# A gated delta layer on one core: conv taps read from PSUM, and VectorE in GpSimd's place for the weights' low parts and the silu products

## The chip, the core and the metric

The kernel runs on one core of one Trainium2 chip. The metric is device time in microseconds (us) of one execution. Before the change the median of three runs is 1683.63 us (1683.09 to 1684.1).

## The reference

Two decoder blocks run one after the other on 256 tokens of width 1024. The first prepends 16 meta tokens (272 columns in the kernel) and has two layers: a gated delta layer and an mLSTM layer, each followed by a feed-forward part with a short conv. The second has a feed-forward part, three mixers and another feed-forward part. The change touches the gated delta layer alone:

```python
def gated_deltanet(h, valid, w_in, conv_w, a_log, dt_bias, norm_w, w_out):
    proj = h @ w_in
    qkv = jax.nn.silu(causal_depthwise_conv(proj[..., :o1], conv_w)).astype(f32)
    z = proj[..., o1:o2]
    beta = jax.nn.sigmoid(proj[..., o2:o3])
    g = -jnp.exp(a_log) * jax.nn.softplus(proj[..., o3:] + dt_bias)
    ...
    sol = lax.linalg.triangular_solve(a_mat, rhs, left_side=True, lower=True)
    ...
    _, o = lax.scan(step, S0, xs)
    o = rms_norm(o, norm_w) * jax.nn.silu(z)
    return o.reshape(B, L, GDN_VAL_DIM) @ w_out
```

`w_in` is 1024 x 6176: 1024 columns for the queries, 1024 for the keys, 2048 for the values, 2048 for the gate z, and 32 for beta and g. The conv has 4 taps and runs along the tokens, for each channel by itself.

## The kernel before

Activations lie with channels on the partitions and tokens along the free axis. A product with a weight matrix keeps float32 accuracy with three float32r matmuls: each weight piece is split into a high part `wh` (a rounding copy by ScalarE) and a low part `wl` (the rest, a subtraction by GpSimd or VectorE), the activations likewise, and TensorE adds high by high, high by low and low by high in PSUM (`linear_g`, line 403). A load (`wload`, line 355) is one DMA of 512 KB into `wraw`, the copy that makes `wh`, and the subtraction that makes `wl`. There are three buffers each of `wraw`, `wh` and `wl`, so a load starts when the one three before it has been used.

In the delta layer `linear_g` is called for 256 columns at a time: two PSUM tiles `ps`, two loads of four 128-row pieces each, 24 matmuls a load. The pool has two `ps` buffers. 32 loads make the queries, keys and values (`gdn_proj`, line 971) in four groups of heads, 16 loads make z (`gdn_z`), and a small one the gates. In this layer GpSimd makes `wl` in two halves of 128x512, but for the first two loads, which `embed` prefetches for VectorE.

`conv4` (line 955) turns a `ps` tile into silu of the conv: ScalarE copies `ps` to `cx` in SBUF and writes the last tap to `cy`; VectorE adds the other three taps from `cx` (128x271, 128x270, 128x269); ScalarE takes tanh (`cth`); and the product (1 + tanh) y goes to `kv`, by VectorE in one instruction for the channel tiles 0 to 13 and by GpSimd in two (`cth`, then `kv`) for tiles 14 to 31. The `ps` buffer is free again when ScalarE has read it twice.

Beside the projections run the chunks of the delta rule, on four lanes: `unit_kq` normalises keys and queries (small VectorE chains `rq_*`, then `kqtok` on ScalarE), `gdn_pre` makes the decays (`dp`, `kk`, `BA`), `gdn_core` inverts a triangular matrix by levels (`wy_inverse`: matmul `yp`, ScalarE `Y`, matmuls `w`, VectorE `RT`, then `zp`, `Z`, `r2p`) and updates the state, `gdn_onorm` normalises the output (`on`, `otp`), and `gdn_tail` does the last 16 tokens for all heads (`wp`, `up`, `vnp`, `rsp`). When all is done, the output projection `ps<-og` begins. It ends the layer.

The order of TensorE's instructions is fixed when the program is built: each of these pieces is a generator that yields the tiles it waits for, and a planner (`Threads`, line 114) with costs for each engine picks the piece that could go on first by its reckoning. The other engines run in the order that the tile scheduler gives them. Every engine takes its instructions strictly in that order. `seg` counts the later parts of the network and is 0 in the delta layer; `ordered` and `mixing` are false there.

Of the kernel before, what the change touches and what calls it, by code (L numbers as in the profile page):

```python
# [8 lines left out]
F32 = mybir.dt.float32  # L9
# [5 lines left out]
ALU = mybir.AluOpType  # L15
# [6 lines left out]
T = S + NM  # L22
KD = D // 128
# [62 lines left out]
class Event:  # L86


    def __init__(self):
        self.on = False  # L90
        self.v = None
# [117 lines left out]
class Kern:  # L209
    def __init__(self, ctx, tc, ins, out):  # L210
        self.tc, self.nc, self.ctx = tc, tc.nc, ctx
        nc = tc.nc
        self.th = Threads()
        self.mem_done, self.half = Event(), Event()
        self.pause = [Event() for _ in range(3)]
        self.mwt = {}
        self.ready = {}
        self.V, self.A, self.PE, self.G = (self.th.engine(*e) for e in (
            ("V", nc.vector), ("A", nc.scalar), ("PE", nc.tensor), ("G", nc.gpsimd)))
        self.SY = nc.sync  # L220
        self.i = ins
        self.out = out

        self.const = self.pool(ctx, "const", 1)
        self.p_raw = self.pool(ctx, "praw", 3)
        self.p_hl = self.pool(ctx, "phl", 3)
        self.p_x = self.pool(ctx, "px", 8)
        self.p_h = self.pool(ctx, "ph", 14)
        self.p_s = self.pool(ctx, "psm", 2)
        self.p_t = self.pool(ctx, "ptiny", 2)  # L230
        self.lane = None
        self.ordered = False
        self.mixing = False
        self.near_load = self.seg = 0
        self.mid = None
        self.gctx = ExitStack()
        self.pp = self.pool(self.gctx, "pq", 2, space=PSUM)
        self.p_v = self.pool(self.gctx, "pkvg", 8)
        self.p_l = self.pool(self.gctx, "plane", 1)
        self.p_lp = self.pool(self.gctx, "planep", 1, space=PSUM)  # L240
# [37 lines left out]
        return t  # L278

    def ps(self, shape=(128, T), name="ps"):  # L280
        return self.pp.tile(list(shape), F32, tag="pp", name=name)

    def pcore(self, shape=(128, 4, 128), name="pcs"):
        return self.pc.tile(list(shape), F32, tag="pc", name=name)
# [72 lines left out]
    def wload(self, w, k0, nk, c0, nc_, pieces=1, late=None, own=None, eng=None):  # L357

        key = w.tensor.name, k0, c0
        if key in self.ready:  # L360
            return self.ready.pop(key)
        tile = own or (lambda name, dt: (self.p_raw if name == "wraw" else self.p_hl).tile(
            [128, nk, nc_], dt, tag=name, name=name))
        r = tile("wraw", F32)
        self.A.ahead = self.V.ahead = self.G.ahead = True
        h, l = tile("wh", F32R), tile("wl", F32R)
        self.SY.dma_start(
            r[:], w[k0 * 128:(k0 + nk) * 128, c0:c0 + nc_].rearrange("(k p) c -> p k c", p=128))
        self.nload = getattr(self, "nload", 0) + 1
        every = POOL_EVERY[self.seg]  # L370
        if eng is not None:
            pass
        elif not self.ordered or self.mixing or self.nload <= self.near_load or every and self.nload % every == 0:
            eng, pieces = self.nc.gpsimd if self.ordered or self.mixing else self.G, 2
        else:
            eng = self.V
        sub = [(slice(k, k + nk // pieces), slice(None)) for k in range(0, nk, nk // pieces)] if nk >= pieces else [
            (slice(None), slice(c, c + nc_ // pieces)) for c in range(0, nc_, nc_ // pieces)]
        inst = self.A.copy(h[:], r[:])

        def low():
            for a, b in sub:
                eng.tensor_tensor(l[:, a, b], r[:, a, b], h[:, a, b].bitcast(F32), ALU.subtract)  # L383

        if late is None:
            low()
        else:
            if self.ordered:
                self.order(inst)
            late.append(low)  # L390
        self.A.ahead = self.V.ahead = self.G.ahead = False
        return h, l
# [406 lines left out]
    def embed(self):  # L799

        self.hst = self.cst([128, KD, T], name="hst")
        self.hs = [self.hst[:, k, :] for k in range(KD)]
        f = self.xt
        ss = self.cst([128, 2, 3], name="ss0")
        st = self.tiny([128, 2, 6], "ss1")
        mv = self.tiny([128, 2], "ss2")
        w = self.i["gdn_w_in"][0]
        X = self.xslots()

        def prefetch(*a):  # L810
            late = []
            self.ready[w.tensor.name, a[0], a[2]] = self.wload(w, *a, eng=self.V, late=late)
            return late

        with self.tc.manual_schedule(engines={mybir.EngineType.DVE}):
            self.V.memset(ss[:], 1.0)
            self.V.memset(ss[:, 1, 1:2], 0.0)
            for t in (2, 0):
                for n in range(2):
                    P = TT[t][1]  # L820
                    junk = self.vslot((128, 512), F32, "junk")
                    self.act(junk[:P], f[t][n][:P], AF.Square, accum_out=ss[:P, n, t:t + 1])
            for n in range(2):
                self.V.bn_stats(st[:, n, :], f[1][n][:])
            self.lane = "u1"
            p = self.plane("warm", (128, 512))
            for _ in range(35):
                self.mm(p[:], self.zero[:, :128], self.zero[:])
            self.lane = None
            self.V.bn_aggr(mv[:], st[:])  # L830
            self.stt(ss[:, 0, 1:2], mv[:, 0:1], mv[:, 0:1], mv[:, 1:2], ALU.mult, ALU.add)
            self.ts(ss[:, 0, 1:2], ss[:, 0, 1:2], float(D), ALU.mult)
            self.tt(ss[:, 0, :], ss[:, 0, :], ss[:, 1, :], ALU.add)
            self.ss = ss
            r = self.rsqrt_small([128, 3], ss[:, 0, :], D, EPS)
            rd = self.vslot((128, 3, 128), F32, "rd")
            for t, (o, P) in enumerate(TT):
                self.ts(rd[:P, t, :P], self.ident[:P, :P], r[:P, t:t + 1], ALU.mult)
            self.columns(self.norms, 0)
            low = {1: prefetch(0, KD, 6144, 32), 3: prefetch(0, 4, 1024, 256), 6: prefetch(4, 4, 1024, 256)}  # L840
            self.masks()
            for k in range(KD):
                self.lane = k % 4
                p = self.plane("xp", (128, T))
                for t, (o, P) in enumerate(TT):
                    self.mm(p[:, o:o + P], f[t][k // 4][:P, (k % 4) * 128:(k % 4) * 128 + 128], rd[:P, t, :P], t == 0, True)
                self.act(X[k][0], p[:], AF.Copy, scale=self.pv(k))
                self.stt(X[k][1], p[:], self.pv(k), X[k][0].bitcast(F32), ALU.mult, ALU.subtract)
                for fn in low.get(k, ()):
                    fn()  # L850
            self.lane = None
        self.th.add([self.residual()])
        return X
# [101 lines left out]
    def conv4(self, ps, ct, out):  # L955

        w = lambda j: self.pv(PV_GC + j * 32 + ct)
        y = self.sm(name="cy")
        x = self.p_l.tile([128, T], F32, tag="cx", name="cx", bufs=3)
        self.A.copy(x[:], ps)  # L960
        self.act(y[:], ps, AF.Copy, scale=w(3))
        for s in (1, 2, 3):
            self.stt(y[:, s:], x[:, :T - s], w(3 - s), y[:, s:], ALU.mult, ALU.add)
        th = self.sm(name="cth", tag="th")
        self.act(th[:], y[:], AF.Tanh, scale=0.5)
        if ct >= 14:
            self.tt(th[:], th[:], y[:], ALU.mult, self.G)
            self.tt(out, th[:], y[:], ALU.add, self.G)
        else:
            self.stt(out, th[:], 1.0, y[:], ALU.add, ALU.mult)  # L970

    def gdn_proj(self, X, g):
        W = self.i["gdn_w_in"][0]
        qs, ks, v0, v1 = (self.vslot() for _ in range(4))
        for base, dst in ((1024 + g * 256, ks), (g * 256, qs), (2048 + g * 512, v0), (2304 + g * 512, v1)):
            yield from self.linear_g(W, base, 256, KD, X, T, lambda m, p: self.conv4(p, base // 128 + m, dst[:, m, :]))
        tl = slice(256, T)
        self.G.tensor_copy(self.kqtail[:, 0, 2 * g:2 * g + 2, :], ks[:, :, tl])
        self.G.tensor_copy(self.kqtail[:, 1, 2 * g:2 * g + 2, :], qs[:, :, tl])
        for n, v in enumerate((v0, v1)):  # L980
            self.G.tensor_copy(self.vtail[:, 4 * g + 2 * n:4 * g + 2 * n + 2, :], v[:, :, tl])
        return qs, ks, (v0, v1)
# [1468 lines left out]
```

## Time and profile before

| | us |
|---|---|
| median of three runs | 1683.63 |
| the profiled execution, its own time | 1685.52 |
| its span, first to last instruction | 1683.7 |
| span up to the first projection `ps<-xhl` | 24.3 |
| from there to the first `ps<-og` (the delta layer) | 341.2 |
| the rest | 1318.2 |

The profile names instructions as `output<-inputs` with their shapes. PE is TensorE's matmuls, PEld its weight loads, DVE VectorE, ACT ScalarE, POOL GpSimd. A row's busy time is that of a group; "idle before" is the time in which its engine stood still just before it, and the releaser is what ended that. Nearly all compute instructions bear line 190, that of the helper that records them, so groups are told apart by tile names.

### The profile page before, as it was taken

The page shows a single profiled execution, that of the slowest core. Times are in us where ns is not written, and L with a number is a line of the kernel's source. Part 1 is how long each engine was busy: PE and PEld are TensorE (multiplying, and loading weights), DVE is VectorE, ACT ScalarE, POOL GpSimd, SP SyncE. Part 2 cuts the span into 40 slices and gives each one's busy share as a digit, 9 for nine tenths or more (in the row PEclk, how much of TensorE's full clock was granted, in tenths as well). Part 3 has the DMA queues.
Part 4 walks back from the last instruction along what each step waited for, and adds up shares of the span by engine and source line. Part 5 has one row for each costly group of instructions (what it writes and reads, how often), then busy time and mean ns, then how long its engine had stood idle before and what let it go on. Part 6 is the DMA issues. An engine that isn't in the chain of part 4 may idle for free.

```text
span 1683.7 us, 31234 instructions
## 1 busy us (share of the span) xinstructions
PE 1557.9 (93%) x11939; PEld 1470.2 (87%) x11939; DVE 1141.3 (68%) x2284; ACT 936.2 (56%) x1893; POOL 576.6 (34%) x531
## 2 busy tenths in 40 slices
PE   8889888999799997999799998999997899999999
PEld 6778778899799996888788998999986789999987
DVE  5788878766988758448977667554659564466643
ACT  4567766655566544447566646454544655564542
POOL 3674554320200002450334441112265547612221
PEclk9899999999999999999899999999998999999999
DMA  5331221236355553335346554556654335656664
GB/s 157 88 89 53 75 63 55 72 110 196 113 171 169 175 175 101 91 114 151 118 156 190 170 181 150 176 178 197 184 149 128 101 93 151 186 158 184 184 191 150
DMA packets 239100, 235.40 MB, mean 140 GB/s; under 512 B 11510, under 2 KB 226406, under 8 KB 238950
## 3 DMA queue, kind: packets, MB, share of 16 engines
q1 hardware_dynamic: 238326, 231.86, 46.1%
q8 instruction: 94, 1.54, 0.4%
q0 software_dynamic: 496, 1.41, 0.3%
q14 instruction: 56, 0.46, 0.1%
q10 hardware_dynamic: 128, 0.13, 0.0%
HBM read 232.32 MB, written 1.05 MB: 139 GB/s over the span
## 4 chain that ended last, share of the span: by engine, by line
PE 39%; DVE 9%; DMA 3%; ACT 3%; issue 1%; POOL 1%; ACTq 0%; POOLq 0%; DVEq 0%
PE ps L190 31%; PE pst L190 5%; ACT wh L190 1%; DVE wl L190 1%; PE memp L190 1%; DVE fy L190 1%; DVE rq_a L190 1%; DMA wraw<-in_ffn_w_up_dram 1%; DMA wraw<-in_ml_w_out_dram 1%; DVE rq_y L190 1%; DMA wraw<-in_mem_w_kv_dram 1%; POOL wl L383 1%; DVE qtok L190 1%; DVE qsq L190 1%; PE rsp L190 0%
## 5 line engine op out<-in xcount | busy, mean ns | idle before, releaser
L190 ACT CAST wh<-wraw 128x1024 fp32r<-128x1024 f32 (+2 forms) x436 | 447.9, 1029 | 392.2 <-PE ps L190 249.8
L190 PE MATMUL ps<-xhl,wh 128*128 128x272 f32 (+2 forms) x3280 | 639.8, 295 | 19.7 <-DVE py L190 8.3
L383 POOL TENSOR_TENSOR wl<-wraw,wh 128x512 fp32r<-128x512 f32 (+3 forms) x262 | 333.4, 1296 | 666.4 <-ACT wh L190 616.1
L190 PEld LDWEIGHTS ps<-xhl,wh 128*128 128x128 f32 x3280 | 514.5, 192 | 25.9 <-DVE py L190 8.7
L190 PE MATMUL ps<-xhl,wl 128*128 128x272 f32 (+2 forms) x1640 | 465.1, 288 | 0.8 <-POOL wl L383 0.8
L190 DVE TENSOR_TENSOR wl<-wraw,wh 128x1024 fp32r<-128x1024 f32 (+3 forms) x239 | 289.1, 1210 | 180.8 <-ACT wh L190 176.2
L190 PEld LDWEIGHTS ps<-xhl,wl 128*128 128x128 f32 x1640 | 312.2, 192 | 1.2 <-POOL wl L383 1.2
L190 PE MATMUL ps<-xr,wh 128*128 128x256 f32 (+2 forms) x1216 | 225.3, 293 | 25.0 <-DVE py L190 23.0
L190 POOL TENSOR_TENSOR wl<-wraw,wh 128x512 fp32r<-128x512 f32 x132 | 172.4, 1327 | 162.7 <-ACT wh L190 154.5
L190 PEld LDWEIGHTS ps<-xr,wh 128*128 128x128 f32 x1216 | 191.8, 197 | 27.7 <-DVE py L190 18.2
L190 PE MATMUL ps<-hh,wh 128*128 128x256 f32 (+1 forms) x1056 | 190.8, 283 | 0.0
L190 PE MATMUL ps<-xr,wl 128*128 128x256 f32 (+2 forms) x608 | 164.1, 291 | 1.1 <-DVE wl L190 1.1
L190 PEld LDWEIGHTS ps<-hh,wh 128*128 128x128 f32 x1056 | 163.1, 188 | 0.0
L190 PE MATMUL ps<-hh,wl 128*128 128x256 f32 (+1 forms) x528 | 149.8, 284 | 0.4 <-DVE wl L190 0.4
L190 PEld LDWEIGHTS ps<-xr,wl 128*128 128x128 f32 x608 | 114.0, 196 | 1.6 <-DVE wl L190 1.5
L190 PEld LDWEIGHTS ps<-hh,wl 128*128 128x128 f32 x528 | 99.6, 189 | 0.6 <-DVE wl L190 0.6
L190 DVE SCALAR_TENSOR_TENSOR cy<-cx,pvt,cy 128x271 f32<-128x271 f32 (+2 forms) x96 | 74.5, 779 | 13.5 <-ACT cy L190 12.5
L190 DVE SCALAR_TENSOR_TENSOR fy<-ps,pvt,fy 128x256 f32<-128x256 f32 (+2 forms) x128 | 62.4, 488 | 17.4 <-ACT fy L190 16.0
L190 DVE TENSOR_TENSOR hh<-fy,hh 128x256 fp32r<-128x256 f32 (+1 forms) x88 | 63.8, 728 | 11.7 <-ACT hh L190 11.6
L190 DVE TENSOR_TENSOR py<-ps,rstd 128x256 f32<-128x256 f32 (+2 forms) x96 | 39.9, 423 | 37.8 <-PE ps L190 37.5
L190 POOL MEMSET mvt<- 128x4 f32 x4 | 0.4, 102 | 182.9 <-PE ps L190 182.9
L190 ACT CAST hh<-fy 128x256 fp32r<-128x256 f32 (+1 forms) x88 | 35.7, 408 | 38.4 <-DVE fy L190 37.8
(537 smaller groups left out, 2650.8 us busy)
## 6 DMA issues: line engine op xcount, KB each, us to landing
wraw<-in_ffn_w_up_dram SPq DMA_DIRECT2D x88, 512.0 KB
wraw<-in_ffn_w_gu_dram SPq DMA_DIRECT2D x88, 512.0 KB
wraw<-in_ffn_w_down_dram SPq DMA_DIRECT2D x79, 512.0 KB
wraw<-in_gdn_w_in_dram SPq DMA_DIRECT2D x48, 512.0 KB
wraw<-in_w_in_dram SPq DMA_DIRECT2D x41, 512.0 KB
wraw<-in_ml_w_in_dram SPq DMA_DIRECT2D x24, 512.0 KB
wraw<-in_gdn_w_out_dram SPq DMA_DIRECT2D x16, 512.0 KB
wraw<-in_ml_w_out_dram SPq DMA_DIRECT2D x8, 512.0 KB
```

Of the source, the lines that this page charges most:

```text
L190: r = f(*args, **kw)
L383: eng.tensor_tensor(l[:, a, b], r[:, a, b], h[:, a, b].bitcast(F32), ALU.subtract)
```

## The change

Four edits. `conv4` no longer copies `ps` to `cx`: the three taps read `ps` itself; and all 32 products are made by VectorE in one instruction. In `wload`, `wl` is made by VectorE in one piece of 128x1024 wherever `seg` is 0 and no engine was named; later parts keep their rules. `gdn_proj` calls `linear_g` for 128 columns at a time: one `ps` tile, one load of eight 128-row pieces of 128 columns, 24 matmuls; the prefetched loads follow. And before each such tile the generator yields the key of the buffer that it takes (`free`), so that the planner reckons with the time at which the tile two before was read.

```diff
     def ps(self, shape=(128, T), name="ps"):
-        return self.pp.tile(list(shape), F32, tag="pp", name=name)
+        t = self.pp.tile(list(shape), F32, tag="pp", name=name)
+        self.taken.append(t.tensor.name)
+        return t
+
+    def free(self, t):
+
+        n = self.taken.index(t.tensor.name)
+        key = f"pp{n % 2}"
+        self.th.bank[key] = self.taken[n - 2] if n > 1 else None
+        return key
...
-            eng, pieces = self.nc.gpsimd if self.ordered or self.mixing else self.G, 2
+            eng, pieces = (self.nc.gpsimd, 2) if self.ordered or self.mixing else (self.V, 1) if self.seg == 0 else (self.G, 2)
...
-            low = {1: prefetch(0, KD, 6144, 32), 3: prefetch(0, 4, 1024, 256), 6: prefetch(4, 4, 1024, 256)}
+            low = {1: prefetch(0, KD, 6144, 32), 3: prefetch(0, KD, 1024, 128), 6: prefetch(0, KD, 1152, 128)}
...
-        x = self.p_l.tile([128, T], F32, tag="cx", name="cx", bufs=3)
-        self.A.copy(x[:], ps)
         self.act(y[:], ps, AF.Copy, scale=w(3))
         for s in (1, 2, 3):
-            self.stt(y[:, s:], x[:, :T - s], w(3 - s), y[:, s:], ALU.mult, ALU.add)
+            self.stt(y[:, s:], ps[:, :T - s], w(3 - s), y[:, s:], ALU.mult, ALU.add)
         th = self.sm(name="cth", tag="th")
         self.act(th[:], y[:], AF.Tanh, scale=0.5)
-        if ct >= 14:
-            self.tt(th[:], th[:], y[:], ALU.mult, self.G)
-            self.tt(out, th[:], y[:], ALU.add, self.G)
-        else:
-            self.stt(out, th[:], 1.0, y[:], ALU.add, ALU.mult)
+        self.stt(out, th[:], 1.0, y[:], ALU.add, ALU.mult)
...
-            yield from self.linear_g(W, base, 256, KD, X, T, lambda m, p: self.conv4(p, base // 128 + m, dst[:, m, :]))
+            for m in range(2):
+                ps = self.ps((128, T))
+                yield [self.free(ps)]
+                yield from self.linear_g(W, base + m * 128, 128, KD, X, T,
+                                         lambda _, p: self.conv4(p, base // 128 + m, dst[:, m, :]), [ps])
```

Three places show what this does to the order of instructions. The first is VectorE at the head of the layer, while the gates' chain (`lp`, ending in `gg`) runs between the first convs. Before:

```order
L190 TENSOR_TENSOR ba<-ba,db 128x3x16
L190 TENSOR_SCALAR lp<-lp 128x96
L190 RECIPROCAL lp<-lp 128x96
L190 SCALAR_TENSOR_TENSOR cy<-cx,pvt,cy 128x271
L190 TENSOR_TENSOR lp<-lp 128x96
L190 SCALAR_TENSOR_TENSOR cy<-cx,pvt,cy 128x270
L190 TENSOR_TENSOR lp<-lp 128x96
L190 SCALAR_TENSOR_TENSOR cy<-cx,pvt,cy 128x269
L190 TENSOR_SCALAR lp<-lp 128x96
```

With the change:

```order
L190 TENSOR_TENSOR ba<-ba,db 128x3x16
L190 TENSOR_TENSOR wl<-wraw,wh 128x1024
L190 SCALAR_TENSOR_TENSOR cy<-ps,pvt,cy 128x271
L190 TENSOR_SCALAR lp<-lp 128x96
L190 SCALAR_TENSOR_TENSOR cy<-ps,pvt,cy 128x270
L190 RECIPROCAL lp<-lp 128x96
L190 SCALAR_TENSOR_TENSOR cy<-ps,pvt,cy 128x269
L190 TENSOR_TENSOR wl<-wraw,wh 128x1024
L190 TENSOR_TENSOR lp<-lp 128x96
```

The taps read `ps`, and two `wl` now stand in VectorE's queue between the first step of the gates and the rest of their chain.

The second is GpSimd in the same layer, from the last of the constants (`lvl`) on. Before:

```order
L190 CAST lvl<-ctmp 128x4x128 x2
L190 TENSOR_TENSOR wl<-wraw,wh 128x512 x8
L190 COPY kqtail<-kv 128x32
L190 TENSOR_TENSOR wl<-wraw,wh 128x512 x2
L190 COPY kqtail<-kv 128x32
L190 TENSOR_TENSOR wl<-wraw,wh 128x512 x4
L190 TENSOR_TENSOR cth<-cth,cy 128x272
L190 TENSOR_TENSOR kv<-cth,cy 128x272
```

With the change:

```order
L190 CAST lvl<-ctmp 128x4x128 x2
L190 COPY kqtail<-kv 128x32 x2
L190 COPY vtail<-kv 128x32 x2
L190 COPY kqtail<-kv 128x32
L190 AFFINE_SELECT BA<-BA 128x256
L190 CAST Br<-BA 128x256
L190 AFFINE_SELECT BA<-BA 128x256
L190 TENSOR_TENSOR Bl<-BA,Br 128x256
```

What is left to GpSimd here are small copies and the first steps of the inverses (`BA`, `Br`, `Bl`).

The third is TensorE at the end of the layer. Before, 16 triples of z's projection (`ps<-xhl`) stand between the last matmul of the tail (`rsp`) and the output projection; the last rows of them, and its beginning:

```order
L190 MATMUL ps<-xhl,wh 128x272 x2
L190 MATMUL ps<-xhl,wl 128x272
L190 MATMUL ps<-xhl,wh 128x272 x2
L190 MATMUL ps<-xhl,wl 128x272
L190 MATMUL ps<-og,wh 128x272 x2
L190 MATMUL ps<-og,wl 128x272
```

With the change, the last rows before it:

```order
L190 MATMUL r2p<-RT,Z 128x128
L190 MATMUL otp<-eye,on 128x128 x2
L190 MATMUL wp<-R_5119,kbg 128x128 x2
L190 MATMUL otp<-eye,on 128x128 x2
L190 MATMUL up<-R_5119,bv 128x128 x2
L190 MATMUL up<-wq,St 128x2x16 x16
L190 MATMUL otp<-eye,on 128x128 x2
L190 MATMUL vnp<-eye,vnT 128x128 x2
L190 MATMUL up<-BA,vn 128x128 x2
L190 MATMUL rsp<-sq,ones 128x256
L190 MATMUL ps<-og,wh 128x272 x2
L190 MATMUL ps<-og,wl 128x272
```

No projection is left for the tail: the last `ps<-xhl` stands ahead of three `yp` levels of an inverse, of the last core's state and output, and of the whole tail, with nothing but these behind it until `ps<-og`. From the output projection on, TensorE's instructions are the same in both.

## Rows read from the trace of the kernel before

**Rows 1.** Busy time by engine in the delta layer, 24.3 to 365.5 us.
```profile
core 0: us, PE busy (x) PEld busy (x) DVE busy (x) ACT busy (x) POOL busy (x), PEclk, DMA share, GB/s
24.30:365.50 341.20, 295.70 (x2437) 270.57 (x2437) 263.43 (x629) 220.79 (x664) 181.65 (x196) 0.95 0.26 74
```
**Rows 2.** Waits of PE in the layer: us in total, times, longest.
```profile
PE yp L190 <- DVE RT L190: 13.1, 10, 3.3
PE kqp L190 <- ACT kqtok L190: 6.7, 4, 3.5
PE gp L190 <- DVE gg L190: 5.2, 1, 5.2
PE otp L190 <- DVE on L190: 5.0, 3, 4.4
```
**Rows 3.** Groups by shape, DVE and POOL, in the layer: busy us, mean ns, idle before.
```profile
L190 DVE SCALAR_TENSOR_TENSOR cy<-cx,pvt,cy 128x271 f32<-128x271 f32 x32 | 28.6, 893 | 12.5 <-ACT cy L190 12.5
L190 DVE SCALAR_TENSOR_TENSOR cy<-cx,pvt,cy 128x270 f32<-128x270 f32 x32 | 23.5, 733 | 0.5
L190 DVE SCALAR_TENSOR_TENSOR cy<-cx,pvt,cy 128x269 f32<-128x269 f32 x32 | 22.8, 713 | 0.6
...
L190 DVE TENSOR_TENSOR rq_a<-rq_a,rq_v 128x4 f32<-128x4 f32 x24 | 8.1, 347 | 0.3
...
L190 POOL TENSOR_TENSOR wl<-wraw,wh 128x512 fp32r<-128x512 f32 x92 | 121.1, 1337 | 93.0 <-ACT wh L190 84.8 <-PE w L190 7.0 <-PE otp L190 1.2
L190 POOL TENSOR_TENSOR kv<-cth,cy 128x272 f32<-128x272 f32 x18 | 14.5, 806 | 0.8
```
**Rows 4.** Single tiles in the layer: duration ns min/median/max, first and last start.
```profile
L190 DVE SCALAR_TENSOR_TENSOR cy<-cx,pvt,cy x96: 477/520/1571, 32.6 to 254.9; 128x271 f32<-128x271 f32 x32, 128x270 f32<-128x270 f32 x32, 128x269 f32<-128x269 f32 x32
L190 DVE SCALAR_TENSOR_TENSOR kv<-cth,cy x14: 421/434/1526, 37.9 to 230.8; 128x272 f32<-128x272 f32 x14
L190 DVE TENSOR_TENSOR rq_a<-rq_a,rq_v x39: 143/161/1222, 75.8 to 342.9; 128x4 f32<-128x4 f32 x24, 128x8 f32<-128x8 f32 x12, 128x2 f32<-128x2 f32 x3
L190 DVE TENSOR_SCALAR on<-on,rq_o x32: 273/276/1322, 171.8 to 346.7; 128x128 f32<-128x128 f32 x32
```
**Rows 5.** Order of time on DVE (start us, us) beside two of POOL's `wl`.
```profile
33.92 1.33 DVE L190 TENSOR_TENSOR lp<-lp 128x96 f32<-128x96 f32 x1
35.18 1.53 DVE L190 SCALAR_TENSOR_TENSOR cy<-cx,pvt,cy 128x269 f32<-128x269 f32 x1
...
33.56 2.85 POOL L190 TENSOR_TENSOR wl<-wraw,wh 128x512 fp32r<-128x512 f32 x2 [0.43 <-ACT wh L190]
```
**Rows 6.** Groups by shape, DVE, from 365.5 to 800 us, after the layer.
```profile
L190 DVE TENSOR_TENSOR wl<-wraw,wh 128x1024 fp32r<-128x1024 f32 x89 | 108.9, 1224 | 52.6 <-ACT wh L190 51.1 <-PE ps L190 0.2
L190 DVE SCALAR_TENSOR_TENSOR fy<-ps,pvt,fy 128x271 f32<-128x271 f32 x32 | 15.8, 495 | 0.0
```
**Rows 7.** Groups by shape, ACT, in the layer.
```profile
L190 ACT CAST wh<-wraw 128x1024 fp32r<-128x1024 f32 x47 | 49.3, 1049 | 9.5 <-POOL wl L190 4.8 <-PE ps L190 2.3 <-issue 2.1
L190 ACT COPY cx<-ps 128x272 f32<-128x272 f32 x32 | 12.4, 389 | 3.3 <-PE ps L190 3.2
```
**Rows 8.** Waits of ACT for weights from memory, 0 to 450 us.
```profile
ACT wh L190 <- DMA wraw<-in_gdn_w_in_dram: 2.0, 3, 1.1
```
**Rows 9.** Order of time on PE at the layer's end, and its projections there.
```profile
331.32 0.28 PE L190 MATMUL w<-Y,RT 128*128 128x128 f16 x2
...
333.17 0.28 PE L190 MATMUL yp<-RT,Br 128*128 128x128 f16 x2
334.86 0.29 PE L190 MATMUL w<-Y,RT 128*128 128x128 f16 x2
...
346.50 1.06 PE L190 MATMUL wp<-R,kbg 128*128 128x128 f32 x4
...
365.51 0.55 PE L190 MATMUL ps<-og,wh 128*128 128x272 f32 x2
...
346.50:365.50 19.00, 12.70 (x85) 11.32 (x85) 1.29 (x3) 0.79 (x2) 0.94 0.27 84
```

More of the change, by code (lines that the diff above doesn't have):

```diff
@@ L231, in __init__ @@
         self.lane = None
+        self.taken = []
         self.ordered = False
```

## The prediction

> **What bounds the kernel now.** I read the busy time by stretch first, then the waits of TensorE, then the groups of instructions. The change moves instructions between 24.3 us and the first output projection at 365.5 us; TensorE's rows are the same after that, so only these 341.2 us are in question. There PE is busy 295.7 us, and DVE 263.4, more than ACT (220.8) and POOL (181.7) [rows 1]. PE thus stands still some 45 us in the layer, and its waits name the cause: 13.1 us for VectorE's `RT`, 6.7 for `kqtok` behind the small `rq` chains, 5.2 for `gg` at the end of the gates' chain, 5.0 for `on` [rows 2]. None of these four is a wait for a weight or for a `ps` buffer. They are steps of the delta rule that come late through VectorE's queue, so the layer is set by how soon VectorE gets to them, and by what projections TensorE has in hand meanwhile.
>
> Part of VectorE's busy time is no work. The three taps from `cx` have the same size within two columns, yet take 893, 733 and 713 ns on average [rows 3] with a minimum of 477 and a maximum of 1571 [rows 4]. An `rq_a` of 4 columns takes 347 ns on average [rows 3], against 161 at the median and up to 1222 [rows 4]. The order of time shows how: an `lp` of 96 columns takes 1.33 us and the next tap 1.53 us just while GpSimd runs two halves of `wl` [rows 5]. VectorE instructions with their inputs in SBUF stand still until GpSimd's instruction ends. A tap-like instruction that reads PSUM (`fy`, 128x271) takes 495 ns, mean of 32 [rows 6].
>
> **The change on VectorE.** 46 of the 48 large loads now put one `wl` of 128x1024 there, 1.224 us each by the same instruction later on [rows 6]: +56.3 us. The 18 products that GpSimd made in two steps [rows 3] become 18 of 434 ns, the median of VectorE's own 14 [rows 4]: +7.8. The 96 taps fall from 74.9 us in sum [rows 3] to 96 x 0.495 = 47.5 [rows 6]: -27.4. What GpSimd cost the small instructions goes nearly all: for the 24 `rq_a` of one form 24 x (0.347 - 0.161) = 4.5 us [rows 3, 4], about as much again in their sister rows, 6 for the 32 `on` and 5 in the gates' chain, together -20. So VectorE gets 64.1 more and 47.4 less, +17: 263 becomes 280 of 341 us. It is no lighter, but its waits of up to 1.57 us at random places turn into `wl` of 1.22 us at known ones.
>
> [...]
>
> **On the path.** TensorE's instructions are the same in number and shape; what changes is its idle time. Four terms.
>
> (a) Waits relieved: of the 6.7 us for `kqtok`, the share of GpSimd's hindrance in its chain, (347 - 161) / 347 = 54% [rows 3, 4], is 3.6. Of the 5.0 for `on`, 40%, is 2. The 5.2 for `gg` loses some 5 us of hindrance (two such are in [rows 5]) and gains two `wl`, 2.4 us: -3. Of the 13.1 for `RT` I take 3, for VectorE's load is not lighter. Together -12, with ends 0 and -25 (all four waits gone but 5).
>
> (b) TensorE's order. The 85 projection matmuls which now run beside the tail, from `wp` to `ps<-og` [rows 9], stand earlier in the changed order, in front of the lanes' steps. At the layer's pace (24 a load, some 2.95 us) they are 10.4 us; they fill idle time that is there, 45 us, if they fall on it. Taken -10, ends 0 and -10.4.
>
> (c) In return the end is bare. Behind the last projection come three levels of an inverse, at 1.85 us from `w` to `yp` and 1.69 from `yp` to `w` [rows 9] some 3.5 each, 10.6 together; about 2 for the inverse's end; and the tail, 19.0 us as it stands with cover, 8.6 if the 85 matmuls are taken out whole [rows 9]. So between 21 and 32 us. I take 25, nearer the low end, since without cover nothing stands before a step on PE. PE's own work in it is about 9 us. Idle there: +16, ends +12 and +23.
>
> (d) The `ps` buffer is held until the third tap: cast (1.05 us [rows 7]) if it comes first, last tap's product on ACT (0.5), and three taps of 0.5 with a product or a `wl` between, some 3 to 4.5 us, against 24 matmuls of the next tile, 2.95 us. Back to back it would cost up to 1.4 us a tile; it hurts only while nothing but projections is there, about the first nine tiles, 0 to +12 us. The planner now knows of it and puts other work between. Taken 0.
>
> The rest costs nothing: ACT loses 32 copies, 12.4 us [rows 7], on an engine that idles a third of the layer. The DMAs keep their number, 512 KB each, with rows half as long; SP issues them in the same order behind the same buffers. ACT waited 2.0 us for them [rows 8]; 0, with an end of +2 if that doubles. GpSimd's `BA`, `Br` and `Bl` no longer stand behind `wl`: it is in (a)'s upper end.
>
> Sum: -12 - 10 + 16 + 0 = -6 us on the profiled execution's 1685.5 us (span 1683.7 and 1.8 around it), 1679.5. That execution stands 1.9 us above the median of the runs, so the forecast is **1678 us**, 0.3% faster.
>
> **Rivals.** *VectorE's queue becomes the bound (slower).* Each `wl` needs the cast by ACT, which needs the buffer of three loads ago, and everything behind it in VectorE's queue, `RT` above all, waits along. The price is in the trace: 52.6 us idle in front of 89 `wl` later on, 0.59 us each [rows 6], where VectorE has time. Times 46 it is 27 us; if two thirds reach PE, 18, the sum is +12, 1695.5 at the runs' level. It turns to the other side once more than 6 of the 27 us reach PE. For it: VectorE is at 82%, and GpSimd waits 84.8 us for casts in the same role [rows 3]. Against: the layer leaves DVE 60 us to wait in.
>
> *The buffer and the bare end cost their upper ends (slower).* (c) at +23 and half of (d), +6: the sum is +7, 1690.5.
>
> *Lateness goes for good (faster).* If VectorE's steps come when PE reaches them, (a) goes to -24: the sum is -18, 1665.5. For it: PE's waits are all of this kind. Against: VectorE's load is no less.
>
> *Nothing moves.* If the relief only changes which step is late, because the lanes take as long as before, (a) and (b) together are worth what (c) costs: within 3.4 us of 1683.6.
>
> **Chances.** About 0.2%, 3.4 us, is what a measurement can tell from no change here. The forecast has 0.35, the faster rival 0.18, no change 0.15, VectorE's queue 0.22, buffer and bare end 0.10. So 0.53 faster, 0.15 same, 0.32 slower. Cases of both signs hold most of the chance: the forecast's own range is 1671 to 1681, and the whole range, from (a) full with (c) at its low end to the queue's 27 us on the path nearly whole, is 1656 to 1702.
>
> **What would show it.** In the changed profile: taps near 495 ns, no spread up to 1.5 us; `rq_a` near 161 ns; `wl` on VectorE near 1.22 us and DVE busy some 280 us in the layer; POOL under 60. PE's waits for `kqtok`, `gg` and `on` small, a bare end of about 25 us with PE mostly idle, and the first `ps<-og` near 359 us. I am wrong if idle time in front of VectorE's `wl` passes 25 us and PE's waits for `RT` grow, if PE waits long for `ps` buffers, if the bare end is over 32 us, or if the time after the first `ps<-og` changes by more than 2 us.

## The result, and the profile after

The changed kernel takes 1700.28 us (median of 4 runs, 1699.14 to 1702.36) against 1683.36 for the kernel before on the same chip: a ratio of 1.0101, interval 1.0088 to 1.0114. It is 1% slower; 0.3% faster was forecast. The profiled execution has a span of 1697.4 us where before it was 1683.7.

Busy time by engine in the delta layer of the changed kernel, whole (answers to [rows 1]), then up to its last projection matmul, behind it, and in 20 us of that end. The columns are those of [rows 1]:

```profile
22.10:382.80 360.70, 304.56 (x2438) 277.69 (x2436) 259.28 (x698) 217.15 (x636) 34.10 (x68) 0.90 0.27 74
...
22.10:351.40 329.30, 283.11 (x2344) 261.23 (x2342) 245.21 (x653) 205.08 (x608) 34.10 (x68) 0.93 0.28 78
351.40:382.90 31.50, 21.49 (x97) 16.52 (x96) 14.18 (x48) 12.17 (x28) 0.00 (x0) 0.57 0.10 32
360.00:380.00 20.00, 16.00 (x67) 12.58 (x65) 7.91 (x28) 6.06 (x12) 0.00 (x0) 0.50 0.00 1
```

The layer grew from 341.2 to 360.7 us. It has the same matmuls, but PE is busy 304.6 us instead of 295.7 (+8.9) and idle 56.1 instead of 45.5 (+10.6). In the first 329.3 us PE is idle 46.2 us, as long as in the whole layer before. Then comes a bare end of 31.5 us in which TensorE's granted clock is 0.57 of full speed, and 0.50 through 20 us of it.

VectorE's instructions in the changed kernel's layer by shape, then single tiles (they answer to [rows 3] and [rows 4]):

```profile
L190 DVE TENSOR_TENSOR wl<-wraw,wh 128x1024 fp32r<-128x1024 f32 x49 | 60.4, 1233 | 24.8 <-ACT wh L190 24.6
...
L190 DVE SCALAR_TENSOR_TENSOR cy<-ps,pvt,cy 128x271 f32<-128x271 f32 x32 | 15.8, 493 | 0.0
```
```profile
L190 DVE SCALAR_TENSOR_TENSOR cy<-ps,pvt,cy x96: 399/493/500, 29.4 to 247.9; 128x271 f32<-128x271 f32 x32, 128x270 f32<-128x270 f32 x32, 128x269 f32<-128x269 f32 x32
...
L190 DVE TENSOR_TENSOR rq_a<-rq_a,rq_v x39: 145/157/181, 70.3 to 362.9; 128x4 f32<-128x4 f32 x24, 128x8 f32<-128x8 f32 x12, 128x2 f32<-128x2 f32 x3
```

So VectorE does what was forecast of it: taps of 0.49 us with no spread, small chains at their shortest, `wl` of 1.23 us. Its busy time in the layer even falls, from 263.4 to 259.3 us. Yet TensorE waits for it more. PE's waits in the layer (answers to [rows 2]):

```profile
PE kqp L190 <- ACT kqtok L190: 17.8, 6, 6.5
PE gp L190 <- DVE gg L190: 7.1, 1, 7.1
PE yp L190 <- DVE RT L190: 6.1, 6, 1.9
PE ps L190 <- DVE cy L190: 5.2, 5, 2.7
...
PE otp L190 <- DVE on L190: 1.3, 1, 1.3
```

The waits for `RT` and `on` shrank, that for `kqtok` went from 6.7 to 17.8 us. The order of time on VectorE (start us, us) around its longest piece, and what TensorE did next:

```profile
118.94 1.22 DVE L190 TENSOR_TENSOR wl<-wraw,wh 128x1024 fp32r<-128x1024 f32 x1
...
120.83 0.14 DVE L190 TENSOR_TENSOR rq_a<-rq_a,rq_v 128x4 f32<-128x4 f32 x1
120.91 0.48 DVE L190 SCALAR_TENSOR_TENSOR cy<-ps,pvt,cy 128x270 f32<-128x270 f32 x1
...
121.94 1.23 DVE L190 TENSOR_TENSOR wl<-wraw,wh 128x1024 fp32r<-128x1024 f32 x1 [0.41 <-ACT wh L190]
123.08 0.49 DVE L190 SCALAR_TENSOR_TENSOR cy<-ps,pvt,cy 128x269 f32<-128x269 f32 x1
123.49 0.15 DVE L190 TENSOR_TENSOR rq_a<-rq_a,rq_v 128x4 f32<-128x4 f32 x1
...
126.07 0.16 DVE L190 TENSOR_SCALAR rq_y<-rq_y 128x2 f32<-128x2 f32 x1
```
```profile
120.66 0.29 PE L190 MATMUL ps<-xhl,wl 128*128 128x272 f32 x1
127.42 0.90 PE L190 MATMUL kqp<-eye,kqtok 128*128 128x128 f32 x3 [6.47 <-ACT kqtok L190]
```

VectorE is hardly idle in this stretch, 0.41 us before a `wl`. But the small `rq` steps, 0.15 us each, stand one by one between the taps of two tiles and two `wl`, and TensorE's fixed order has put `kqp` next. The next projection could run from 123.6 us on: the second `wl` ends at 123.17, and the third tap of the older tile, the last to read the next buffer, at 123.57. But it stands behind `kqp`, and starts at 133.1. Whether this order or VectorE's extra work is to blame is what the experiments ask.

The end in the order of time on PE (answers to [rows 9]): the tail's first matmul, its slowest group, and the output projection:

```profile
365.35 1.22 PE L190 MATMUL wp<-R,kbg 128*128 128x128 f32 x4
...
368.05 6.87 PE L190 MATMUL up<-wq,St 128*128 128x32 f32 x32
...
382.85 1.12 PE L190 MATMUL ps<-og,wh 128*128 128x272 f32 x2 [3.33 <-ACT og L190]
```

From `wp` to `ps<-og` it is 17.5 us, against 19.0 with 85 projection matmuls in it [rows 9]: taking them out, 10.4 us by the forecast's reckoning, shortened the tail by 1.5. Its matmuls ran at a granted clock of 0.50: the 32 of `up` took 6.87 us, and 3.66 before, where the clock from 350 to 355 us was 1.00.

### The profile page after: what moved, and what is told of

It reads as the page before. It is cut to its first block, busy times and chain, and to the rows that moved or that the text cites. A ratio compares the mean times of both kernels' runs of the same rounds, so it can differ in the third digit from the quotient of the medians.

```text
span 1697.4 us, 31120 instructions
## 1 busy us (share of the span) xinstructions
PE 1562.1 (92%) x11939; PEld 1475.9 (87%) x11939; DVE 1133.2 (67%) x2348; ACT 929.2 (55%) x1861; POOL 430.2 (25%) x403
## 3 DMA queue, kind: packets, MB, share of 16 engines
q1 hardware_dynamic: 254710, 231.86, 46.2%
## 4 chain that ended last, share of the span: by engine, by line
PE 39%; DVE 8%; ACT 3%; DMA 2%; issue 1%; POOL 1%; ACTq 0%; DVEq 0%; POOLq 0%
PE ps L190 31%; PE pst L190 4%; ACT wh L190 1%; PE memp L190 1%; DVE wl L190 1%; DVE fy L190 1%; DVE rq_a L190 1%; DVE rq_y L190 1%; DMA wraw<-in_ffn_w_up_dram 1%; POOL wl L393 1%; DMA wraw<-in_ffn_w_gu_dram 1%; DMA wraw<-in_w_in_dram 0%; DVE qtok L190 0%; PE scp L190 0%; DVE qsq L190 0%
## 5 line engine op out<-in xcount | busy, mean ns | idle before, releaser
L190 DVE TENSOR_TENSOR wl<-wraw,wh 128x1024 fp32r<-128x1024 f32 (+2 forms) x285 | 345.4, 1212 | 208.6 <-ACT wh L190 205.6
L190 PE MATMUL ps<-xr,wh 128*128 128x256 f32 (+2 forms) x1216 | 224.5, 292 | 24.3 <-DVE py L190 22.7
L190 PEld LDWEIGHTS ps<-xr,wh 128*128 128x128 f32 x1216 | 191.2, 196 | 26.6 <-DVE py L190 17.8
L190 POOL TENSOR_TENSOR wl<-wraw,wh 128x512 fp32r<-128x512 f32 x40 | 51.3, 1303 | 68.8 <-ACT wh L190 68.8
L190 PE MATMUL pst<-wh,hh 128*128 128x512 f32 x176 | 54.9, 393 | 0.0
L190 PE MATMUL ps<-og,wh 128*128 128x272 f32 x256 | 50.3, 296 | 3.3 <-ACT og L190 3.3
```

The source lines that it names most:

```text
L190: r = f(*args, **kw)
```

## The experiments

Ratios are against the kernel before on the same chips, where its medians were 1683.2 to 1684.0. "Loads before `wp`" says how many of the 48 large loads of projections TensorE's order has ahead of the tail's first matmul: 44.5 before, 48 (all) with the change.

### First four: the booking, the free step, the low parts alone, the clock

**e1: VectorE makes the low parts, but the planner does not book them.** The change with

```diff
-            ... else (self.V, 1) if self.seg == 0 else ...
+            ... else (self.nc.vector, 1) if self.seg == 0 else ...
```

> The changed kernel, but the planner does not book VectorE's time for the weights' low parts; VectorE still makes them. 'Order': with that booking gone the planner puts the lanes' steps forward again (the tail's wp stands after 44.8 loads' worth of projection matmuls, against 48.0 of 48 in the change and 44.5 before), the bare end goes, the layer ends near 360 us and the time is 1674 to 1685. 'Queue': VectorE's own load makes the lanes late whatever the order, and the time stays at 1694 or more.

1690.86 us, ratio 1.0044 (1.003 to 1.0058): 9 us less than the change, 7 above before, with the same work on the same engines. No bare end is left (0.1 us; 44.8 loads before `wp`). The time lies between the two ranges, so neither 'order' nor 'queue' is right by itself.

**e2: no free step.** The change without `yield [self.free(ps)]`.

> The changed kernel without the yield of the ps buffer's key, so the planner again thinks that a buffer is always free. In its order the first tail step stands even later: all 48 loads of projections come before the last inverse's decays (ep at 48.0 against 46.9 in the change). 'Order': slower than the change, 1705 to 1720, through a longer bare end. 'Queue': VectorE's work is the same, so within 4 us of the change's 1700.

1691.84 us, 1.0052 (1.0032 to 1.0073), also 8 us better than the change, although its bare end is longer, 43.3 us. Neither range holds. So the length of the bare end alone is not what decides.

**e3: the kernel before, with the low parts on VectorE and nothing else.** The `wload` line of the change alone.

> The kernel before with one edit: VectorE makes the low parts in the layer, booked by the planner; taps, products and tiles as before. 'Order': wp stands behind all 48 loads, so a bare end of some 25 to 32 us and 1694 to 1706. 'Queue': VectorE has 56 us more and keeps its taps from cx without GpSimd's hindrance, 1690 to 1706 also; alone it does not tell the two apart, but its partner with the same edit unbooked does.

1690.75 us, 1.0042 (1.0022 to 1.0062): less than half of the change's loss, with all 48 loads before `wp` and a bare end of 27.5 us. The partner with this edit unbooked was not run. Its taps still read SBUF, but beside a GpSimd that has little but the products left:

```profile
L190 DVE SCALAR_TENSOR_TENSOR cy<-cx,pvt,cy x96: 400/494/1076, 31.9 to 236.4; 128x271 f32<-128x271 f32 x32, 128x270 f32<-128x270 f32 x32, 128x269 f32<-128x269 f32 x32
```

Their median, 494 ns, is that of the change's taps from PSUM, 493. So what a tap from PSUM saves is the standing still beside GpSimd.

**e4: the clock in the bare end.** The change with matmuls of zeros, into a buffer that nobody reads, between the last steps:

```diff
+            p = self.ps((128, T))
+            while not tail_done.on:
+                yield [self.th.clk["PE"] + 0.3]
+                self.mm(p[:], self.zero[:, :128], self.zero[:, :T])
```

> The changed kernel with dummy matmuls of zeros put by the planner into TensorE's empty time after the last projection until the tail is done; they compute nothing that is used. The granted clock was 0.57 in the bare end. If the low clock makes a good part of it (up<-wq,St took 6.87 us there against 3.66 before), the clock stays near 1, that row is near 3.7 us, and the time falls by 4 to 8 us to 1692 to 1696. If the lanes' other engines set the end, it stays within 3 us of 1700.

1697.53 us, 1.0088 (1.0061 to 1.0116). Busy time in its end, from the last projection on, and from the order of time on PE the 32 small matmuls of the tail:

```profile
349.40:376.30 26.90, 18.91 (x138) 14.55 (x136) 14.16 (x46) 11.98 (x28) 0.00 (x0) 0.90 0.11 36
```
```profile
365.48 3.66 PE L190 MATMUL up<-wq,St 128*128 128x32 f32 x32
```

With the clock at 0.90 these take 3.66 us instead of 6.87, and the end 26.9 instead of 31.5. So some 4.6 us of the end is the clock. The row came out as the first reading has it, the time did not: the median fell by 2.8, with overlapping ranges, less than the 4 to 8 expected.

### Which part of the change costs

**e5: the low parts back on GpSimd.** The change with

```diff
-            ... else (self.V, 1) if self.seg == 0 else (self.G, 2)
+            ... else (self.G, 2)
```

> The change with the low parts back on GpSimd in two pieces; taps from PSUM, products on VectorE, tile by tile projections and the free step stay. Theory W (VectorE, in order, makes the low parts, so its small operations and with them the lanes wait): 10 us or more below the change, 1680 to 1690, wp first about 330 us after the first projection matmul or earlier. Theory P (the split projections, the PSUM buffers held by the taps and the order they bring are what costs): within 4 us of the change, 1696 to 1704.

1679.21 us, 0.9976 (0.9964 to 0.9989): by its time theory W holds, just under its range. Without that edit the other three are a small gain, and the edit with all that follows from it costs 21 us. VectorE's single tiles in this run, where GpSimd makes 92 halves of `wl`:

```profile
L190 DVE SCALAR_TENSOR_TENSOR cy<-ps,pvt,cy x96: 401/493/502, 32.1 to 243.5; 128x271 f32<-128x271 f32 x32, 128x270 f32<-128x270 f32 x32, 128x269 f32<-128x269 f32 x32
...
L190 DVE TENSOR_TENSOR rq_a<-rq_a,rq_v x39: 143/161/1183, 73.1 to 336.5; 128x4 f32<-128x4 f32 x24, 128x8 f32<-128x8 f32 x12, 128x2 f32<-128x2 f32 x3
```

Taps from PSUM stay at 0.49 us beside GpSimd, with a maximum of 502 ns (1571 from SBUF [rows 4]); `rq_a`, on SBUF, still takes up to 1.18 us, against 0.16 at the median.

**e6: the kernel before with the taps from PSUM alone.** The lines of `x` and `cx` gone, the taps on `ps`.

> The kernel before with the taps read from PSUM alone (no copy by ScalarE); all else as before. Theory W: no loss, 1676 to 1685, as ScalarE is spared 48 copies and each tap is faster. Theory P: the buffers held longer cost, 1688 or more.

1696.83 us, 1.008 (1.0065 to 1.0095). By its time theory P is right. TensorE has a wait that the kernel before has not:

```profile
PE ps L190 <- DVE cy L190: 16.4, 15, 4.6
```

Projections of two tiles take both `ps` buffers and wait for the taps of the two before. The change, tile by tile, has 5.2 us of this, and e2, tile by tile without the free step, 6.9, so it is the split that shortens this wait. That the wait is the whole loss is not shown: TensorE's order is another one in e6, its waits for `kqtok`, `gg` and `on` fell by 13 us together, and its idle time in the layer is 6 us longer in all. No run has these taps in the order of the kernel before. (ScalarE is spared 32 copies, not the 48 of the expectation.)

**e7: the kernel before with all products on VectorE.** The `if ct >= 14` branch gone.

> The kernel before with the 18 products of the value tiles on VectorE alone. Theory W: 18 operations of 0.44 us on VectorE and 36 fewer on GpSimd: 1681 to 1686. Theory P says nothing else here. Over 1690 would mean that any work given to VectorE costs in this stage, not the low parts' waits.

1697.82 us, 1.0089 (1.0074 to 1.0104). No theory explains 14 us for 18 instructions of 0.44 us, with less work for GpSimd.

**e8: e6, e7 and e3 together**, without the split of the projections and the free step.

> The kernel before with taps from PSUM, products and low parts on VectorE, but projections of two tiles and no free step. Theory W: as the kernel before with the low parts alone, 1688 to 1693, the taps giving back at most 3 us. Theory P: if only the split and the free step cost, 1683 or less; if the taps from PSUM cost as well, 1695 to 1700.

1707.95 us, 1.0151 (1.0129 to 1.0173), more than expected, and the slowest of all. TensorE's longest wait here is for the taps, too:

```profile
PE ps L190 <- DVE cy L190: 26.3, 17, 3.4
```

Two new questions: why e7 costs what it does, and whether W means the engine or the order that its booking makes.

### Order or engine

The planner books each VectorE and GpSimd instruction, and TensorE's order depends on it. These runs book one engine and use another, so that TensorE's order stays row for row. The other engines' order is not held: where the low parts change engine, about a third of VectorE's other instructions stand at another place, and that counts as the engine's share.

**e9: the change's order, low parts on GpSimd.**

```diff
-            ... else (self.V, 1) if self.seg == 0 else ...
+            ... (self.nc.gpsimd, 2) if self.ordered or self.mixing or self.seg == 0 else ...
...
+            self.th.note("V", [l], [r, h], nk * nc_, True)
```

> The change with TensorE's order kept row for row (the planner still books each low part on VectorE), but GpSimd makes the low parts in two pieces. Theory order (the order that VectorE's booked 1.1 us give is bad): within 4 us of the change, 1696 to 1703. Theory engine (VectorE, working in order, makes lanes late while it waits for and makes low parts): 1679 to 1686.

1695.82 us, 1.008 (1.005 to 1.011).

**e10: the order of e5, low parts on VectorE**, booked in two halves on GpSimd.

> The mirror of the run before: TensorE's order of the variant with GpSimd's low parts, row for row (still booked on GpSimd), but VectorE makes the low parts. Theory order: 1677 to 1683, as that variant. Theory engine: 1690 to 1700. In between both have a share; the two shares of this and the run before should add up to the 21 us between the change and that variant.

1689.81 us, 1.0046 (1.0031 to 1.0061). The layers of e5, e10 and e9, each whole (columns as in [rows 1]):

```profile
23.20:360.80 337.60, 294.95 (x2438) 270.42 (x2437) 237.28 (x648) 212.68 (x633) 149.64 (x160) 0.94 0.28 77
```
```profile
22.20:366.70 344.50, 294.99 (x2439) 270.06 (x2437) 255.63 (x694) 213.56 (x633) 34.18 (x68) 0.95 0.27 76
```
```profile
22.30:376.20 353.90, 303.98 (x2438) 277.98 (x2436) 244.23 (x652) 216.28 (x636) 148.32 (x160) 0.90 0.27 75
```

With the row of the change above, and idle as the layer less PE's busy time:

| TensorE's order | low parts by | layer | PE busy | PE idle | median |
|---|---|---|---|---|---|
| of e5 | GpSimd (e5) | 337.6 | 295.0 | 42.7 | 1679.2 |
| of e5 | VectorE (e10) | 344.5 | 295.0 | 49.5 | 1689.8 |
| of the change | GpSimd (e9) | 353.9 | 304.0 | 49.9 | 1695.8 |
| of the change | VectorE | 360.7 | 304.6 | 56.1 | 1700.3 |

In the layer the two shares add up: the engine costs 6.9 or 6.8 us, nearly all of it idle time of TensorE; the order costs 16.3 or 16.2, of which 9 are the same matmuls at a lower granted clock (0.90, against 0.94 in e5 and 0.95 in e10) and 7 idle time. By the medians the engine's share is 10.6 or 4.5 and the order's 16.6 or 10.5; they hold the time behind the layer too, and each layer here is that of one execution. Both theories have a share: e9 lies just below the range of 'order', e10 just below that of 'engine'. The wait that grew most shows both too. TensorE's wait for `kqtok`, in e5, e10 and e9:

```profile
PE kqp L190 <- ACT kqtok L190: 2.9, 3, 1.6
```
```profile
PE kqp L190 <- ACT kqtok L190: 6.2, 5, 2.8
```
```profile
PE kqp L190 <- ACT kqtok L190: 12.8, 5, 4.4
```

With 17.8 in the change, the order adds some 10 to 12 us of it and VectorE 3 to 5.

**e11: e7's products in the order of the kernel before** (made by VectorE, booked on GpSimd).

> The kernel before with its TensorE order row for row, but the 18 products of the value tiles on VectorE (still booked on GpSimd). Theory order: 1680 to 1685, the 14 us that the same edit cost with its own order are gone. Theory engine: 1694 to 1699.

1681.49 us, 0.9982 (0.9968 to 0.9997). e7's loss of 14 us is gone: it was its order. The products by themselves gain some 2 us.

**e12: the kernel before, no work changed, another order.**

```diff
-    COST = {..., "V": (0.07, 0.00104), ...}
+    COST = {..., "V": (0.08, 0.00104), ...}
```

> The kernel before with no work changed: only the planner's fixed cost of a VectorE operation goes from 0.07 to 0.08 us, which gives another TensorE order. Theory order: the time moves by 5 us or more, either way (1690 to 1700 if this order, which has all projections issued before the last recurrence step ends, is as bad as the similar ones). Theory engine: within 3 us of before, 1681 to 1687.

1702.45 us, 1.0119 (1.0104 to 1.0134). A hundredth of a microsecond in the booked cost of a VectorE instruction loses 19 us, as much as the whole change, 15.5 of it in the layer. There PE is busy 302.21 and idle 54.5 us:

```profile
22.90:379.60 356.70, 302.21 (x2444) 276.52 (x2442) 265.85 (x635) 224.76 (x668) 182.71 (x196) 0.93 0.26 75
```

The number holds for the whole kernel, so in this run and in e13 to e18 TensorE's order behind the layer is another one too (426 to 809 of 9406 matmuls stand elsewhere than in the change). That part is in their medians, beside the layer's.

### What in an order costs, and a better version

**e13 to e16: e5's work in four other orders**, each by one number of the same line: VectorE's fixed cost 0.06, 0.05 and 0.04, or its cost of an element 0.00094. Loads before `wp`: 47.0, 44.9, 43.2, 42.2.

> The variant with GpSimd's low parts (1679 us), no work changed: only the planner's fixed cost of a VectorE operation goes from 0.07 to 0.06 us. Its order has 47.0 of the 48 weight loads' projections issued before the last step's first matmul (wp), where the variant has 45.4, before 44.5 and the change 48. Theory end (what counts is how much projection work is left to cover the last step): 3.0 us a load, 1684 to 1692. Theory scatter (each order has its own waits of the lanes, the end tells nothing): anywhere from 1675 to 1700, with no tie to that number.

1676.36 us, 0.9957 (0.994 to 0.9973): 8 us better than theory end allows.

> As the run before with 0.05 us: 44.9 loads before wp. Theory end: 1676 to 1680, a little under the variant. Theory scatter: anywhere from 1675 to 1700.

1678.71 us, 0.9961 (0.9935 to 0.9986).

> As the run before with 0.04 us: 43.2 loads before wp, 4.8 loads or 14 us of projections for the end. Theory end: 1672 to 1679. Theory scatter: anywhere from 1675 to 1700.

1671.92 us, 0.994 (0.9917 to 0.9962).

> As the runs before, but the fixed cost stays at 0.07 us and the cost of a VectorE element goes from 1.04 to 0.94 ns: 42.2 loads before wp, 17 us of projections for the end, as long as the end itself takes. Theory end: 1670 to 1679, the best of the row, unless the projections then outlast the last step. Theory scatter: anywhere from 1675 to 1700.

1669.95 us, **0.9915 (0.9891 to 0.994)**, faster than both kernels. Its layer, with PE idle for 37.3 us (those of e5 and e13 to e15 take 337.6, 334.7, 331.5 and 331.9 us):

```profile
24.10:352.30 328.20, 290.89 (x2427) 267.81 (x2426) 234.71 (x657) 217.06 (x641) 149.12 (x160) 0.95 0.27 77
```

e14 to e16 fall where theory end puts them, to 0.1 us, though e14's runs spread over 23 us; e13 does not. And e12, whose end is bare for 7.2 us much as e13's for 7.6, is 26 us slower than it, with the work of the kernel before. What is left for the end is therefore at most one cost among others.

**e17: e16's order, low parts on VectorE** (booked as in e10).

> TensorE's order of the fastest run so far (e16, 1670), but VectorE makes the low parts: the change's own placement of the work in the best order found. Theory engine share: as with the order of e5 it costs 5 to 11 us, 1675 to 1681, still below the kernel before. If the best order has no slack for it: 1682 to 1690. If the engine costs nothing in a good order: 1668 to 1672.

1685.07 us, 1.0007 (0.9994 to 1.0021). The engine costs 15 us in this order, more than in the others, as the expectation has it for an order with no slack:

```profile
23.70:363.60 339.90, 293.54 (x2426) 268.24 (x2425) 259.94 (x703) 217.83 (x641) 34.55 (x68) 0.95 0.27 74
```

The layer is 11.7 us longer than e16's, PE's idle time 46.4 instead of 37.3.

**e18: the kernel before with e16's booked costs** (43.1 loads before `wp`).

> The kernel before with no work changed, a booked VectorE element at 0.94 instead of 1.04 ns: 43.1 loads before wp (before 44.5). Theory end: 1676 to 1681, so that part of the gain of e16 is the order's alone. If the gain is the new taps' and products': 1683 or more.

1684.39 us, 1.0015 (0.9998 to 1.0032), no gain (its layer takes 341.6 us, before 341.2), and outside what theory end expects. With e13 it makes two misses in five, so that theory falls as a rule. That the gain of e16 comes from the taps and products fits, but e18 and e16 differ in order too, so it is not separated.

## Why the prediction was wrong

**VectorE's own terms: right.** Taps, `wl`, `rq_a` and GpSimd's rest came as forecast, and DVE's sum even at 259 instead of 280 us: by the same sum the small instructions gave back some 40 us, not 20. For the three taps the copy to SBUF buys nothing: the median from PSUM is 493 ns, and 494 from the copy where GpSimd has little to do (e3).

**(a) and (b), the step that failed.** Together they took 22 us of TensorE's idle time away, so some 23.5 were to be left ahead of the bare end. There are 46.2. That faster small instructions make the lanes early was taken for granted. The waits for `RT` and `on` did shrink, by 7.0 and 3.7 us, more than the 3 and 2 taken; but the one for `kqtok`, which was to lose 3.6, grew by 11.1, and that for `gg`, which was to lose 3, by 1.9. For `gg` the chain itself came as reckoned: `gp`, which reads `gg`, starts 15.7 us after the first projection instead of 19.0. That was partly luck: with the low parts on GpSimd it starts after 16.7 us (e5) or 16.1 (e9), so most of the gain is not GpSimd's hindrance gone. And TensorE's new order has 48 projection matmuls ahead of `gp` instead of 84, so it waits longer, 7.6 us in e5 and e9. A chain that ends sooner saves nothing if TensorE is sent to it sooner still.

For `kqtok` the chain did come later. Its tiles before, then with the change (duration ns min/median/max, first and last start):

```profile
L190 ACT ACTIVATE kqtok<-kqp,rq_y x34: 359/373/427, 78.4 to 310.8; 128x128 f32<-128x128 f32 x34
```
```profile
L190 ACT ACTIVATE kqtok<-kqp,rq_y x34: 349/367/398, 75.3 to 336.0; 128x128 f32<-128x128 f32 x34
```

The last of them starts 287 us after the first projection before, and 314 us with the change. It is 281 us in e5, 290 in e10 and 308 in e9, so between e5 and the change TensorE's order makes 24 to 27 us of it and VectorE's low parts 6 to 9. The 85 matmuls of (b) were moved as said; but they did not fill holes, they stood ahead of the lanes' steps, which then came later. The two shares in idle time are measured against e5: some 7 us come from VectorE making the low parts and 7 from TensorE's order.

**(c), mis-sized in its parts.** The bare end took 31.5 us, not 25, at the upper end of the range. Its idle time is 10 us, not 16; but PE's own work in it is 21.5 us, not 9. Part of that is the clock, for which the prediction had no term: 16.0 us of the work ran at 0.50. In e4 the 32 matmuls of `up` fell from 6.87 to 3.66 us; with the 16.0 halved about like these, PE's work in the end would be an estimated 13.5, still above 9. The 8 us between are most of the 9 us by which PE is busier in the change's order, in e9 too. In e4, at 0.90, the end was 4.6 us shorter.

**(d), priced at nothing.** It costs 5.2 us of waits for taps, inside its ends (0 and 12). Without the tile by tile projections and the free step it is 26.3 (e8), and 16.4 with the low parts on GpSimd (e6). The rival that put half of (d) and the upper end of (c) on the path had the sign right and 1690.5 us; but the bare end's idle time was below even its low end, 12, and what it left out are the clock and the idle time ahead of the end.

**The rival that VectorE's queue becomes the bound: half right.** VectorE stands idle 24.8 us in front of `wl`, where 27 were reckoned. But all that the low parts on VectorE cost TensorE is some 7 us of idle time in the change's order and in e5's, not 18, just past the 6 from which it was to decide (9 in the order of e16). Alone it would not have made the change 17 us slower; e3, with the low parts alone, loses 7. And this idle time is no measure of the loss: in e1 it is 28.2 us, and the time 9 us better. The wait for `RT`, which was to grow in this case, fell.

**Beyond the layer.** From the first `ps<-og` on the trace is 3.6 us shorter, more than the 2 that were allowed. The runs tell no effect of the change in that: in the thirteen traces whose TensorE rows are the same from there on, this stretch takes 1311.4 to 1321.0 us.

**The range.** Its low end, 1656, does not follow from its own terms: -25, -10.4 and +12 give some 1660. Nothing hangs on it.

## What to carry to other kernels

Where a planner fixes the order from booked costs, an edit is two edits: the work, and the new order. Measure them apart by booking one engine and using the other, and first move a booked cost by a hundredth with the work unchanged, to see how far the order alone carries the time (here 19 us, when the whole change costs 17). Before small latency chains are given to a freed engine, count what stands between their steps in its queue and where the new order asks for their results, not the engine's busy share.

## What the runs showed of the hardware

The taps that read `ps` in PSUM were not held up by GpSimd's subtractions: 96 of them took 401 to 502 ns beside 92 halves of `wl` (e5), where `rq_a`, with its inputs in SBUF, goes from 143 up to 1183 ns. In the kernel before, 20 taps from SBUF began inside a half of `wl` and at their shortest time would have ended in it with 0.15 us to spare; every one of them ended 0.29 to 0.30 us after it. Not every instruction with its input in SBUF stood still, as the prediction has it: there a `RECIPROCAL` of `lp` ran from 31.98 to 32.73 us inside a half of `wl` that ended at 33.12.

TensorE's granted clock fell after the last projection, with only short matmuls and gaps on PE: in the changed kernel it was 1.00 from 350 to 355 us and 0.50 from 360 to 380, where PE was busy 16.0 of the 20 us. There 32 small matmuls took 6.87 us instead of 3.66. With matmuls of zeros in the gaps the granted clock over the whole end was 0.90, and the same 32 took 3.66 us (e4).

Some orders scatter from one execution to the next: e14's ten runs spread from 1665.92 to 1688.89 us, the change's four over 3.2 us. The traced one of e14, its slowest, has a layer of 331.5 us, shorter than e5's, and 1330.1 us behind it, where the other traces have 1311.2 to 1321.4. So there the excess lies behind the layer, as far as one trace tells; the cause stays open.
